# The relative-position bias tile of a hybrid decoder step: built through DRAM rows at a skewed pitch, first of all, in place of a matmul flip

## The chip, the cores and the metric

The kernel runs on one core of a Trainium2 chip. The metric is the device time in microseconds of one execution. A core has five engines that work side by side on queues of their own: TensorE (PE, matmuls; its weight loads are a lane of their own, PEld), VectorE (DVE), ScalarE (ACT), GpSimd (POOL) and SyncE (SP), which here only issues DMAs. ACT issues some DMAs as well. Each engine takes its instructions in the order of its queue and waits on semaphores of the others.

## The reference

One inference step of a two-layer decoder trunk, for 1024 prompt tokens and 64 sample tokens. Layer 0 is differential attention with eight heads beside a spatial gating MLP; layer 1 is gated linear attention. All inputs are float32. What the change touches is the bias that is added to the scores of layer 0:

```python
def t5_bucket(dist):
    n = jnp.maximum(dist, 0)
    max_exact = N_BUCKETS // 2          # 32 buckets
    nf = jnp.maximum(n, 1).astype(jnp.float32)
    large = max_exact + (jnp.log(nf / max_exact) / math.log(MAX_DISTANCE / max_exact)
                         * (N_BUCKETS - max_exact)).astype(jnp.int32)
    large = jnp.minimum(large, N_BUCKETS - 1)
    return jnp.where(n < max_exact, n, large)

s = jnp.einsum('bqhcd,bkhcd->bhcqk', q, k).astype(jnp.float32)
bias = rel_bias[t5_bucket(q_pos[:, None] - k_pos[None, :])]
s = s + jnp.transpose(bias, (2, 0, 1)).astype(jnp.float32)[None, :, None]
s = jnp.where(causal, s, -jnp.inf)
p = jax.nn.softmax(s, axis=-1)
a = p[:, :, 0] - lam * p[:, :, 1]
```

The bias depends only on the head and on the distance between query and key, and is the same for all distances of 128 and more. So, less its last value (which a softmax doesn't see), it is zero outside a band, and one tile of 128 query rows by 256 keys for each head holds it for every block of queries, with a large negative number where the key lies after the query.

## The kernel before

The prompt is worked in eight tiles of 128 tokens, and the 64 sample tokens are the ninth (NT = 9). Layer 0 starts with a loop over 72 units, head by head and in each head tile by tile (lines 465 to 507). In step s the loop emits the projection of unit s (`qkv_tile`, 24 matmuls), and for earlier units the transposes (2 steps back), the scores (5 back), the softmax times values (6 and 8 back) and the output transposes (12 back). Ahead of the loop stand `xprep` of the first four x tiles (load, normalise, transpose, split in a high and a low part), `load_head(0)` (the weights of head 0, eight DMAs of 192 KB through four buffers) and `small_consts`. `xprep` has two buffers for loaded tiles.

The program's order gives each instruction a priority. A planner with a model of the times (`schedule_with_timeline_sim`) then lays out the queue of each engine: an instruction that is ready in the model may pass one of higher priority that isn't. On the chip the order of a queue is fixed.

The bias tile `tb` (128 partitions x 8 heads x 256) is made by `bias_setup` (lines 208 to 230), called in step s = 1. Three small loads (`rel`, `r31`, `oh`; lines 213 to 215) bring the table, its last row and a one-hot matrix. DVE subtracts (L216), TensorE makes a row of 384 bias values for each head, running from distance 255 down (L218), DVE copies it to SBUF as `bsb`, 8 x 384 (L220), and SP writes it to DRAM as `bias_d` (L221). Two DMAs read it back into `rev` with a step of one element from partition to partition (L226), so partition p holds the row shifted by p. This is `tb` with its partitions in reverse, and a matmul with a reversed identity (`flip`, loaded at L223) turns it round, four times 512 columns (L229), each followed by a DVE copy into `tb` (L230).

`scores` adds `tb` to the scores on DVE (L405). `bias_sample` (L235) copies rows of `tb` into `biasS` for the sample tokens, 16 small DMAs on SP, in steps 20 to 27 of the program.

Of the kernel before, what the change touches and what calls it, by code (L numbers as in the profile page):

```python
# [10 lines left out]
F32 = mybir.dt.float32  # L11
# [13 lines left out]
P = 128  # L25
KT = D // P
H = 8
# [10 lines left out]
PRM = {'ktc': 'a', 'ev': 'p', 'ekm': 'p', 'qem': 'd', 'gm': 2, 'wp': (3, 6), 'at': 'a', 'LQ': 2, 'LS': 5, 'LA': 6, 'L2': 8, 'LO': 12, 'on': 'a', 'oT': 'a', 'qk4': 'p', 'kh': 'd', 'vt': 'a', 'qkc': 'a', 'sq': 'p', 'kg': 'p', 'at0': 'a', 'at1': 'a', 'qh': 'd', 'onm': 'd', 'TS': True, 'p0': 2, 'p1': 2, 'qkb': 3, 'qhb': 2, 'ksb': 3, 'lpq': 2, 'qd': 'a', 'vb': 16, 'atb': 2, 'onb': 4}  # L38
# [18 lines left out]
VL = 3  # L57
NW = 14
KW = 4
LEVELS = (64, 32, 16, 8, 4, 2, 1)  # L60


# [4 lines left out]
def ap_of(a, off, dims):  # L67
    return bass.AP(a.tensor, a.offset + off, dims)
# [3 lines left out]
def hybrid_step(  # L72
# [1 line left out]
    x_prompt, x_sample, cache_k, cache_v, state_gla, page_table, rel_bias, norm0_g, w_in0,  # L74
    q_norm_g, k_norm_g, lam, subln_g, ln_v_g, ln_v_b, spatial_w, spatial_b, w_out0,
    norm1_g, w_in1, w_gate, b_gate, gla_norm_g, w_out1,
    c_f32, c_onehot, c_lev, c_flip,
    y_prompt, y_sample, k_prompt, v_prompt, k_sample, v_sample, vb_sample, gla_prompt, gla_sample,
):
    nc = tc.nc  # L80
    pe, act, dve, pool = nc.tensor, nc.scalar, nc.vector, nc.gpsimd
# [18 lines left out]

    dram = ctx.enter_context(tc.tile_pool(name="dram", bufs=1, space=DRAM))
    oT_d = dram.tile([2 * KT, P, T], F32, name="oT_d")
    bias_d = dram.tile([H, 384], F32, name="bias_d")
    vb_d = dram.tile([T + NS, D], F32, name="vb_d")
    v_d = dram.tile([T, D], F32, name="v_d")
    g_d = dram.tile([T, D], F32, name="g_d")
# [9 lines left out]
    cf = const([P, 326], "cf")  # L116
# [66 lines left out]
    if True:  # L183
# [24 lines left out]
        def bias_setup(pp, ps, tb):  # L208
            rel = pp.tile([33, H], F32, name="rel", bufs=1)
            r31 = pp.tile([32, H], F32, name="r31", bufs=1)  # L210
            oh = pp.tile([33, 384], F32, tag="on", name="oh", bufs=PRM["onb"])
            dve.memset(rel[32:33, :], BIG)
            nc.sync.dma_start(rel[0:32, :], rel_bias)
            nc.sync.dma_start(r31, rel_bias[31:32, :].broadcast_to([32, H]))
            nc.sync.dma_start(oh, c_onehot)
            dve.tensor_tensor(rel[0:32, :], rel[0:32, :], r31, ALU.subtract)  # L216
            bps = ps.tile([P, 512], F32, tag="t", name="bps", bufs=3)
            pe.matmul(bps[:H, :384], rel, oh, start=True, stop=True)  # L218
            bsb = pp.tile([H, 384], F32, tag="on", name="bsb", bufs=PRM["onb"])
            dve.tensor_copy(bsb, bps[:H, :384])  # L220
            nc.sync.dma_start(bias_d, bsb)  # L221
            flip = pp.tile([P, P], F32, tag="on", name="flip", bufs=PRM["onb"])
            nc.sync.dma_start(flip, c_flip)  # L223
            for q in range(2):
                rev = pp.tile([P, 4, 256], F32, tag="p1", name=f"rev{q}", bufs=PRM["p1"])
                nc.sync.dma_start(rev, ap_of(bias_d, q * 4 * 384, [[1, P], [384, 4], [1, 256]]))  # L226
                for u in range(2):
                    bps = ps.tile([P, 512], F32, tag="t", name=f"bfl{q}_{u}", bufs=3)
                    pe.matmul(bps, flip, rev[:, u * 2:u * 2 + 2, :], start=True, stop=True)  # L229
                    dve.tensor_copy(tb[:, q * 4 + u * 2:q * 4 + u * 2 + 2, :].rearrange("p h k -> p (h k)"), bps)  # L230

        def bias_sample(tb, h):
            for c in range(2):
# [27 lines left out]
        with ExitStack() as p1:  # L261
            pa = p1.enter_context(tc.tile_pool(name="pa", bufs=2))
            ps = p1.enter_context(tc.tile_pool(name="ps1", bufs=2, space=PSUM))
# [27 lines left out]
            def xprep(i):  # L291
                r = rows(i)
                xt = pa.tile([P, D], F32, tag="xt", name=f"xt{i}", bufs=2)
                nc.sync.dma_start(xt[:r], x_rows(i))
                if i == 0:
                    nc.scalar.dma_start(gbc, norm0_g.broadcast_to([P, D]))
                    nc.sync.dma_start(cf, c_f32)
                xn = pa.tile([P, D], F32, tag="at", name=f"xn{i}", bufs=PRM["atb"])
                ss = pa.tile([P, 1], F32, tag="ss0", name=f"ss0_{i}")
                act.activation(xn[:r], xt[:r], AF.Square, accum_out=ss[:r])  # L300
                rs = pa.tile([P, 1], F32, tag="rs0", name=f"rs0_{i}")
                rsqrt(rs[:r], ss[:r], 1, 1.0 / D)
                dve.scalar_tensor_tensor(xn[:r], xt[:r], rs[:r], gbc[:r], ALU.mult, ALU.mult)
                for half in range(2):
                    tp = ps.tile([P, 512], F32, tag="t", name=f"xtp{i}_{half}", bufs=3)
                    tv = tp.rearrange("p (k t) -> p k t", k=4)
                    for k in range(4):
                        kk = half * 4 + k
                        pe.transpose(tv[:, k, :r], xn[:r, kk * P:(kk + 1) * P], ident[:r, :r])
                    o = (i % 3) * P  # L310
                    hs = xh[i // 3][:, half * 4:half * 4 + 4, o:o + r]
                    ls = xl[i // 3][:, half * 4:half * 4 + 4, o:o + r]
                    split(hs, ls, tv[:, :, :r])
                    if i == NT - 1:
                        pool.tensor_copy(xs[:, half * 4:half * 4 + 4, :NS], f32(hs))
                        pool.tensor_copy(xs[:, half * 4:half * 4 + 4, NS:], f32(ls))
# [136 lines left out]
            def load_head(h):  # L453
                Ws[h] = load_w(w_in0, 0, [(s * D + h * P, P) for s in range(3)], f"wq{h}", PRM['lpq'] if h else 4)

            wp = ps.tile([P, 512], F32, tag="t", name="wp", bufs=3)
            for _ in range(NW):
                pe.matmul(wp[:, :P], ones, ones, start=True, stop=True)
            xprep(0)
            load_head(0)  # L460
            xprep(1)
            small_consts()
# [22 lines left out]
            for s in range(len(units) + max(8, PRM['LO'] + 1)):  # L485
                if s == len(units) - 2:
                    load_gate(0)
                stage(s, PRM['LO'], otr)
                stage(s, PRM['L2'], av2)
                stage(s, PRM['LA'], av)  # L490
                stage(s, PRM['LS'], scores)
                stage(s, PRM['LQ'], qk_trans)
                if 0 <= s - 1 < len(units) and units[s - 1][1] == NT - 1:
                    stage(s, 1, qkv_post)
                if 1 <= s <= NT - 4:
                    xprep(s + 3)
                if s == 1:
                    bias_setup(pa, ps, tb)
                if 20 <= s < 20 + H:
                    bias_sample(tb, s - 20)  # L500
                if s < len(units):
                    h, i = units[s]
                    if i == 3 and h + 1 < H:
                        load_head(h + 1)
                    st_[h, i] = qkv_tile(h, i, Ws[h])
                elif s - len(units) < NPRE:
                    gate_a(*du[s - len(units)], gate_tiles)
# [384 lines left out]
    with ExitStack() as p4:  # L892
# [516 lines left out]
        for n in range(NT - 1):  # L1409
            tb = TB[n]  # L1410
# [28 lines left out]
def _constants():  # L1439
    cf = np.zeros((P, 326), np.float32)  # L1440
    cf[:, 0:P] = np.eye(P)
    for h in range(H):
        for c in range(2):
            for q in range(8):
                r = (h % 4) * 32 + (h // 4) * 16 + c * 8 + q
                cf[r, 128 + (h % 4) * 32 + (h // 4) * 8 + q] = 1.0
                cf[r, 320 + c] = 1.0
    b = np.arange(NS) // 8
    cf[:NS, 256:320] = b[:, None] == b[None, :]
    part = np.arange(P) // 8 % 4  # L1450
    cf[:, 322] = np.where(part == 1, -1.0, 1.0)
    cf[:, 323] = part == 1
    cf[:, 324] = np.where(part == 2, -1.0, 1.0)
    cf[:, 325] = part == 2
    n = np.arange(256)
    nf = np.maximum(n, 1).astype(np.float32)
    large = 16 + (np.log(nf / np.float32(16)) / np.float32(math.log(8.0)) * np.float32(16)).astype(np.int32)
    bucket = np.where(n < 16, n, np.minimum(large, 31))
    oh = np.zeros((33, 384), np.float32)
    for e in range(384):  # L1460
        dist = 255 - e
        oh[bucket[dist] if dist >= 0 else 32, e] = 1.0
    lev = np.zeros((P, len(LEVELS), 64), np.int32)
    s = np.arange(P)[:, None]
    for li, hf in enumerate(LEVELS):
        m = np.arange(64)[None, :]
        t = (m // hf) * 2 * hf + hf + m % hf
        lev[:, li, :] = (s // (2 * hf) == t // (2 * hf)) & (s % (2 * hf) < hf)
    return {"c_f32": cf, "c_onehot": oh, "c_lev": lev, "c_flip": np.ascontiguousarray(np.eye(P, dtype=np.float32)[::-1])}


_INS = ["x_prompt", "x_sample", "cache_k", "cache_v", "state_gla", "page_table", "rel_bias", "norm0_g", "w_in0",
# [23 lines left out]
```

## Time and profile before

| what | value |
|---|---|
| median of 3 runs | 1801.37 us (1799.54 to 1802.87) |
| profiled execution, span from first to last instruction | 1806.1 us |
| instructions | 31855 |
| PE busy | 1747.1 us, 97% |
| DVE busy | 1012.4 us, 56% |
| ACT busy | 755.4 us, 42% |
| POOL busy | 609.3 us, 34% |
| mean granted TensorE clock | 0.991 of full |

No time beside its span is given for the profiled execution; the span is 4.7 us above the median. Times below are from the start of the span. [...] In the timeline, a number in brackets is how long the engine was idle before the instruction, with what ended that.

### The profile page before, as it was taken

The numbers are of one execution on the slowest core, as the hardware profiler recorded it, in microseconds if no ns is written. First come the engines' busy times: TensorE is split into PE (matmuls) and PEld (weight loads), VectorE is DVE, ScalarE is ACT, GpSimd is POOL, SyncE is SP. The second block draws the span as 40 slices with busy tenths as digits, with TensorE's granted clock in tenths as the row PEclk, the third lists the DMA queues.
The fourth block names the chain that finished last, engine by engine and source line by source line (L and its number), as shares of the span: only waits on it lengthen the run. The fifth ranks groups of instructions, "written<-read, shape, count | busy, mean of one in ns | idle before, by whom it ended". The sixth has DMA issues, their size and how long they took to land.

```text
span 1806.1 us, 31855 instructions
## 1 busy us (share of the span) xinstructions
PE 1747.1 (97%) x11429; PEld 1629.0 (90%) x11429; DVE 1012.4 (56%) x2223; ACT 755.4 (42%) x1934; POOL 609.3 (34%) x893
## 2 busy tenths in 40 slices
PE   7999999999999899999899999999999999998999
PEld 6798999999999888889899999999999999996777
DVE  5898888988983233223832342444354455667442
ACT  4566656666664222223222232333343334345241
POOL 4555646655653221112721200044111232235230
PEclk8999999999999999999999999999999999999999
DMA  7102202211213766746221262432334244438741
GB/s 211 52 23 73 68 20 67 67 43 43 66 59 104 243 202 232 236 165 213 59 79 54 92 199 74 129 97 82 94 116 152 80 126 123 130 111 260 240 130 71
DMA packets 223302, 211.62 MB, mean 117 GB/s; under 512 B 22286, under 2 KB 201143, under 8 KB 223143
## 3 DMA queue, kind: packets, MB, share of 16 engines
q1 hardware_dynamic: 203510, 194.35, 34.7%
q10 hardware_dynamic: 19632, 15.21, 2.8%
q8 instruction: 91, 1.49, 0.4%
q14 instruction: 69, 0.56, 0.1%
HBM read 151.35 MB, written 56.24 MB: 115 GB/s over the span
## 4 chain that ended last, share of the span: by engine, by line
PE 62%; DVE 16%; DMA 9%; ACT 4%; POOL 4%; issue 4%; SPq 0%; ACTq 0%; POOLq 0%; DVEq 0%
PE o L1373 5%; PE yo L143 3%; PE yo L145 3%; PE yo L144 3%; PE vg L143 3%; PE vg L144 3%; PE vg L145 3%; DMA oT_d<-oTr 2%; DVE p L418 2%; PE zv L143 1%; PE zv L144 1%; PE zv L145 1%; PE o L434 1%; PE s L399 1%; PE qkv L143 1%
## 5 line engine op out<-in xcount | busy, mean ns | idle before, releaser
L412 ACT ACTIVATE p<-s,nm 128x256 f32<-128x256 f32 (+7 forms) x128 | 95.0, 747 | 38.3 <-DVE nm L409 22.3
L399 PE MATMUL s<-ks,qs 128*128 128x512 f32 (+3 forms) x384 | 96.5, 364 | 2.8 <-DVE ks L384 1.4
L87 ACT CAST qs<-qs 64x256 fp32r<-64x256 f32 x128 | 51.7, 404 | 76.8 <-DVE qs L381 74.2
L1120 POOL TENSOR_TENSOR e<-e,k 128x256 f32<-128x256 f32 (+1 forms) x50 | 42.4, 853 | 117.1 <-ACT e L1117 100.8
L338 POOL TENSOR_TENSOR sq<-qk 128x256 f32<-128x256 f32 (+1 forms) x72 | 46.9, 652 | 95.0 <-ACT qk L87 94.2
L434 PE MATMUL o<-v,at 128*128 128x128 f32 x576 | 76.8, 279 | 1.6 <-ACT at L87 1.6
L399 PEld LDWEIGHTS s<-ks,qs 128*128 128x128 f32 x384 | 64.9, 190 | 12.6 <-ACT p L412 2.8
L434 PEld LDWEIGHTS o<-v,at 128*128 128x128 f32 x576 | 71.4, 193 | 4.2 <-ACT at L87 2.6
L131 POOL TENSOR_TENSOR s<-s,mhalf 128x4 f32<-128x4 f32 (+1 forms) x72 | 73.3, 1018 | 5.3
L837 DVE TENSOR_TENSOR yp<-yp,yo 128x384 f32<-128x384 f32 (+1 forms) x48 | 25.3, 530 | 74.5 <-ACT yp L836 41.7
L407 DVE TENSOR_REDUCE nm<-s 128x1 f32<-128x640 f32 (+3 forms) x64 | 65.2, 1019 | 1.2
L747 POOL TENSOR_TENSOR u<-u,th 128x384 f32<-128x384 f32 (+1 forms) x24 | 28.7, 1194 | 99.9 <-DVE th L746 99.4
L405 DVE TENSOR_TENSOR s<-s,tb 128x256 f32<-128x256 f32 (+1 forms) x128 | 52.8, 412 | 8.9 <-PE s L399 5.6
L418 DVE SCALAR_TENSOR_TENSOR p<-p,fac,p 128x128 f32<-128x128 f32 (+3 forms) x64 | 55.1, 861 | 1.7
L1373 PE MATMUL o<-w1h,oh 128*128 128x512 f32 x128 | 53.0, 414 | 2.5 <-ACT oh L1350 2.5
L87 ACT COPY at<-atp 128x512 f32<-128x512 f32 (+2 forms) x96 | 44.5, 481 | 20.0 <-PE atp L427 19.8
L746 DVE SCALAR_TENSOR_TENSOR th<-th,gb 128x384 f32<-128x384 f32 (+1 forms) x24 | 12.6, 524 | 69.0 <-ACT th L745 69.0
L1373 PE MATMUL o<-w1l,oh 128*128 128x512 f32 x128 | 50.8, 397 | 0.0
L1373 PE MATMUL o<-w1h,ol 128*128 128x512 f32 x128 | 50.3, 407 | 0.0
L427 PE MATMUL atp<-cf,p 128*128 128x128 f32 x288 | 46.8, 275 | 1.9 <-DVE p L418 1.8
L343 POOL TENSOR_TENSOR qk<-qk,s 128x256 f32<-128x256 f32 (+1 forms) x72 | 46.6, 647 | 4.7
L381 DVE SCALAR_TENSOR_TENSOR qs<-qkt,qg,qs 64x128 fp32r<-64x128 f32 x128 | 44.5, 348 | 3.6
(825 smaller groups left out, 6340.4 us busy)
## 6 DMA issues: line engine op xcount, KB each, us to landing
kp<-in_cache_k SPq DMA_DIRECT2D x32, 512.0 KB
vp<-in_cache_v SPq DMA_DIRECT2D x32, 512.0 KB
or<-oT_d SPq DMA_DIRECT2D x16, 384.0 KB
vb_d<-zs SPq DMA_DIRECT2D x36, 128.0 KB
oT_d<-ob SPq DMA_DIRECT2D x8, 544.0 KB
gt<-g_d SPq DMA_DIRECT2D x34, 128.0 KB
xt<-in_x_prompt SPq DMA_DIRECT2D x8, 512.0 KB
out<-v ACTq DMA_DIRECT2D x64, 64.0 KB
```

Source lines behind the costliest of these rows:

```text
L87: act.activation(o, i_, AF.Copy, scale=scale) if scale is not None else act.copy(o, i_)
L131: pool.tensor_tensor(dst, dst, mhalf[:dst.shape[0], :n], ALU.pow)
L143: pe.matmul(out, lh, rh, start=(s == 0), stop=False)
L144: pe.matmul(out, lh, rl, start=False, stop=False)
L145: pe.matmul(out, ll, rh, start=False, stop=(s == n - 1))
L399: pe.matmul(sc[c][:, k0:k0 + w], qs[:, c, l], kts[h, j][:, c, :w], start=(l == 0), stop=(l == 1))
L405: dve.tensor_tensor(sc[c][:, lo:n], sc[c][:, lo:n], tb[:, h, 256 - (n - lo):], ALU.add)
L407: dve.tensor_reduce(nm[:, c:c + 1], sc[c][:, :n], axis=AX.X, op=ALU.max, negate=True)
L412: act.activation(pc[:, :n], sc[c][:, :n], AF.Exp, bias=nm[:, c:c + 1], accum_out=ss[:, c:c + 1])
L418: dve.scalar_tensor_tensor(pt[0][:, :n], pt[1][:, :n], fac, pt[0][:, :n], ALU.mult, ALU.add)
L434: pe.matmul(op[:, :P], at[:, j * P:(j + 1) * P], vts[h, j], start=(j == 0), stop=(j == i))
L1373: pe.matmul(it.mp[:r], lh[:, k, :r], rh[k][:, cs], start=(k == 0 and a == 0), stop=(k == KT - 1 and a == 2))
```

## The change

The row `bsb` is written to DRAM 128 times for each head, one copy behind the other at a pitch of 385 elements (SH), in one DMA from ACT's queue whose source repeats. One DMA on SP's queue then reads `tb` at a pitch of 384, beginning at element 127: partition p begins at 127 + 384 p, which is element 127 - p of copy p. So the tile arrives the right way round, and the flip, its constant, its four pairs of matmuls and the four copies are gone. `bias_setup` is called right after `xprep(0)`, ahead of `load_head(0)`, in place of step s = 1.

```diff
+SH = 385
-    bias_d = dram.tile([H, 384], F32, name="bias_d")
+    bias_d = dram.tile([H, P * SH], F32, name="bias_d")
             bsb = pp.tile([H, 384], F32, tag="on", name="bsb", bufs=PRM["onb"])
             dve.tensor_copy(bsb, bps[:H, :384])
-            nc.sync.dma_start(bias_d, bsb)
-            flip = pp.tile([P, P], F32, tag="on", name="flip", bufs=PRM["onb"])
-            nc.sync.dma_start(flip, c_flip)
-            for q in range(2):
-                rev = pp.tile([P, 4, 256], F32, tag="p1", name=f"rev{q}", bufs=PRM["p1"])
-                nc.sync.dma_start(rev, ap_of(bias_d, q * 4 * 384, [[1, P], [384, 4], [1, 256]]))
-                for u in range(2):
-                    bps = ps.tile([P, 512], F32, tag="t", name=f"bfl{q}_{u}", bufs=3)
-                    pe.matmul(bps, flip, rev[:, u * 2:u * 2 + 2, :], start=True, stop=True)
-                    dve.tensor_copy(tb[:, q * 4 + u * 2:q * 4 + u * 2 + 2, :].rearrange("p h k -> p (h k)"), bps)
+            nc.scalar.dma_start(ap_of(bias_d, 0, [[P * SH, H], [SH, P], [1, 384]]), bsb[:, None, :].broadcast_to([H, P, 384]))
+            nc.sync.dma_start(tb, ap_of(bias_d, 127, [[SH - 1, P], [P * SH, H], [1, 256]]))
@@
             xprep(0)
+            bias_setup(pa, ps, tb)
             load_head(0)
@@
-                if s == 1:
-                    bias_setup(pa, ps, tb)
```

## Rows read from the trace of the kernel before

**Rows 1.** The page: busy us, share of the span and instructions of each engine.
```profile
PE 1747.1 (97%) x11429; PEld 1629.0 (90%) x11429; DVE 1012.4 (56%) x2223; ACT 755.4 (42%) x1934; POOL 609.3 (34%) x893
```

**Rows 2.** Windows of 10 us: length, busy PE, PEld, DVE, ACT, POOL; clock, DMA share, GB/s.
```profile
10.00:20.00 10.00, 8.61 (x44) 7.16 (x43) 9.23 (x20) 7.80 (x17) 3.75 (x6) 0.83 0.91 254
20.00:30.00 10.00, 9.24 (x59) 8.97 (x58) 7.36 (x11) 6.00 (x14) 7.99 (x12) 1.00 0.76 227
30.00:40.00 10.00, 8.45 (x38) 7.20 (x36) 4.40 (x6) 2.06 (x5) 5.64 (x12) 0.83 0.28 83
40.00:50.00 10.00, 7.28 (x14) 3.21 (x14) 2.79 (x5) 0.49 (x3) 0.04 (x1) 0.66 0.47 131
50.00:60.00 10.00, 9.96 (x64) 9.93 (x65) 9.07 (x23) 6.16 (x14) 6.82 (x13) 1.00 0.10 28
```

**Rows 3.** The chain that ended last, around the bias tile: start, us, what.
```profile
34.35 4.11 DMA bias_d<-bsb
38.48 4.01 DMA rev<-bias_d
```

**Rows 4.** Timeline of the engines, 6 to 58 us: start, us, engine, line, operation.
```profile
6.13 1.06 ACT L300 ACTIVATE xn<-xt 128x1024 f32<-128x1024 f32 x1 [3.38 <-DMA xt<-in_x_prompt]
10.93 0.62 PE L143 MATMUL qkv<-wq0h,xh 128*128 128x384 f32 x1 [0.24 <-ACT xh L135]
19.01 0.44 PE L144 MATMUL qkv<-wq0l,xh 128*128 128x384 f32 x1 [0.59 <-DVE wq0l L175]
33.68 0.45 PE L143 MATMUL qkv<-wq0h,xh 128*128 128x384 f32 x1 [1.24 <-ACT v L87]
34.25 1.53 DVE L303 SCALAR_TENSOR_TENSOR xn<-xt,rs,gbc 128x1024 f32<-128x1024 f32 x1
42.62 6.62 PE L229 MATMUL bfl<-rev,flip 128*128 128x512 f32 x8 [2.94 <-DMA rev<-bias_d]
49.09 0.27 PE L364 MATMUL qkt<-cf,qk 128*128 128x128 f32 x1
57.30 0.28 DVE L405 TENSOR_TENSOR s<-s,tb 128x128 f32<-128x128 f32 x1
```

**Rows 5.** SP's queue in order of time, DMA issues: start, us, line, transfer, count.
```profile
1.72 2.62 SPq L172 DMA_DIRECT2D wq0r<-in_w_in  x4
10.04 1.81 SPq L172 DMA_DIRECT2D wq0r<-in_w_in  x3
11.89 0.47 SPq L213 DMA_DIRECT2D rel<-in_rel_bias  x1
15.14 0.36 SPq L294 DMA_DIRECT2D xt<-in_x_prompt  x1
39.51 0.58 SPq L294 DMA_DIRECT2D xt<-in_x_sample  x1
45.42 7.62 SPq L235 DMA_DIRECT2D biasS<-tb  x11
```

**Rows 6.** Groups by line, first 60 us: count, busy us, mean ns of one.
```profile
L216 DVE TENSOR_TENSOR rel<-rel,r 32x8 f32<-32x8 f32 x1 | 1.0, 997 | 0.0
L218 PE MATMUL bps<-oh,rel 33*8 33x384 f32 x2 | 0.8, 484 | 0.0
L220 DVE COPY bsb<-bps 8x384 f32<-8x384 f32 x1 | 0.5, 536 | 0.0
```

**Rows 7.** DMA view: ACT's queue (q10) in 730.4:731 and 703.65:704.5; the copy's size.
```profile
q10 hardware_dynamic: 13, 0.03, 13.7%
...
q10 hardware_dynamic: 9, 0.03, 14.0%
...
vn<-vsm ACTq DMA_DIRECT2D x8, 32.0 KB
```

**Rows 8.** DMA view of 2 to 6 us: queue, packets, MB, share of 16 engines.
```profile
q1 hardware_dynamic: 288, 0.63, 45.8%
q10 hardware_dynamic: 144, 0.52, 35.6%
```

More of the change, by code (lines that the diff above doesn't have):

```diff
@@ L76, in hybrid_step @@
     norm1_g, w_in1, w_gate, b_gate, gla_norm_g, w_out1,
-    c_f32, c_onehot, c_lev, c_flip,
+    c_f32, c_onehot, c_lev,
     y_prompt, y_sample, k_prompt, v_prompt, k_sample, v_sample, vb_sample, gla_prompt, gla_sample,
@@ L1468, in _constants @@
         lev[:, li, :] = (s // (2 * hf) == t // (2 * hf)) & (s % (2 * hf) < hf)
-    return {"c_f32": cf, "c_onehot": oh, "c_lev": lev, "c_flip": np.ascontiguousarray(np.eye(P, dtype=np.float32)[::-1])}
+    return {"c_f32": cf, "c_onehot": oh, "c_lev": lev}
 _INS = ["x_prompt", "x_sample", "cache_k", "cache_v", "state_gla", "page_table", "rel_bias", "norm0_g", "w_in0",
```

## The prediction

> **What bounds the kernel now.** I read the page first, then the windows of the first 60 us, the SP queue in order of time, the chain of waits and the DMA view of short stretches. TensorE is busy for 97% of the span [rows 1], so a change outside it counts only where it stops or starts that engine. The windows show where it is not full: 8.61, 9.24, 8.45 and 7.28 us of each ten between 10 and 50 us, and 9.96 from 50 on [rows 2]. The bias tile sits in the worst of these. After the matmul, the 8x384 row goes to DRAM (4.11 us from issue to the next step), comes back as 128 shifted rows (4.01 us), and only then the flip matmuls start [rows 3]. [...] From 39.68 (42.62 less 2.94) to 49.09 it does nothing but this: 9.4 us. DVE, ACT and POOL are busy for 2.79, 0.49 and 0.04 us of that window [rows 2]: they wait for TensorE and have nothing that would step into its place.
>
> **What is removed.** The 9.4 us as a whole. Its successors were ready: the transposes of the first tile need a POOL result of long before, and the projection of tile 4 follows 1.4 us behind them in either kernel. DVE's four copies lay in its own idle time and are no gain of their own. The flip's 64 KB load goes too; I cost it at nothing, as SP waits for the written row right after it. In 30 to 40 us the clock is 0.83 [rows 2]; whether that slow piece stays is open, between 0 and 1.5 us of gain (0.17 of 10 us). I take 0.
>
> **What is moved.** The three small loads now go out before the head's weights: 0.47 us of SP time for one [rows 5], some 1.4 for the weights and the second x tile. The first weight load was issued at 1.72 [rows 5] and ACT's first work on anything loaded is at 6.13 [rows 4], so DMA, not SP, sets this start; cost 0, or 1.4 without that cover. The subtraction (1.0 us on DVE), the two matmuls (0.97) and the copy (0.54) [rows 6] fall before 10 us, where DVE is ahead of its first x tile and TensorE has only warm-up: cost 0, or 0.5 if the copy comes just ahead of the x normalisation. The row is then in SBUF near 9.5 us (loads landed with the first x tile near 6.5, plus 2.5).
>
> **What is added, first the write.** ACT's queue writes 8 x 128 x 384 floats, 1.57 MB, where SP wrote 12 KB. Nothing in the trace has this shape, so I bound it. From below: the rate of a full stretch, 254 GB/s in 10 to 20 us [rows 2], makes 6.2 us. The nearest row is the sample values' copy, 32 KB out of eight partitions on the same queue. In one quiet stretch of 0.6 us its packets took 13.7% of 16 engines, 1.3 us of engine time for 32.8 KB, or 25 GB/s for one engine [rows 7]; eight rows going side by side at that rate would make 200 GB/s and 7.9 us. In another it was 14.0% of 0.85 us, 17 GB/s, or 11.4 us. From above: that whole 32.8 KB needed about these 0.6 us, 55 GB/s, and 1.57 MB at that pace needs 28.8 us. I take 8 to 11, because the packets themselves ran at full engine speed in the quiet stretch; the long end stays for the range. With the 4.11 us that even the 12 KB write needed [rows 3], it lands at 22 to 25 us, or 42 at the long end.
>
> [...]
>
> **Then the read and SP's wait.** The tile is read as 1 MB in one DMA. Its halves were read in before too, the first in 4.01 us; 5.5 us for both is my estimate. It lands at 28 to 31 us. Its first reader, DVE's addition to the scores, runs at 57.30 [rows 4], so 47.9 without the 9.4 us: 17 us of room, and none at the long end (48). The new wait is SP's: its read waits for the write, and everything behind it on that queue waits along, x tiles, the last weights of head 0, key stores and the next head's weights. Where it stands in SP's order, the trace tells only indirectly. In before the x load of the sample tile went out at 39.51 [rows 5], though the slot it needed was free when DVE ended its normalisation at 35.78 (34.25 + 1.53) [rows 4]; the read of the bias row stood ahead of it and waited. So the order is made with shorter DMA times than the chip has, and I expect the new read early, among the loads of 10 to 20 us. I take the fourth x tile (issued at 15.14 [rows 5]) as the first one behind it, with the weights of 10.04 to 11.85 as the bad and a later x tile as the good side. Held to 24, it goes out at 25, has the 1 MB ahead of it and lands near 31; from landing to its first projection matmul a tile needs 4.8 us (6.13 to 10.93 [rows 4]), so 36 against 33.68 before [rows 4]: 2.3 us late.
>
> **Sharing of the DMA engines.** Between 2 and 6 us the two queues run side by side (45.8% and 35.6% of the engines [rows 8]). So loads of 12 to 22 us share with the write; 1.57 MB at 254 GB/s is at most 6.2 us for what lies behind all of it, about half of that for head 0's last weights. TensorE has some 2 us of idle between 20 and 34 us to absorb it (0.76 in one window and 1.24 ahead of tile 3 [rows 2, 4]). Left: about 1. This and SP's wait delay the same tiles, so they don't add in full: 3 us for both, from 0 to 6. The 16 small copies into the sample bias (7.62 us of SP time for the first 11 [rows 5]) come earlier; they fall where x tiles have ten and more us of room, cost 0.
>
> **Sum.** 1806.1 - 9.4 + 3.0 = 1799.7 for the span, that is 6.4 less. The median of the runs shown is 4.7 us below the profiled span; I carry the difference over: 1801.4 - 6.4 = **1795.0**. What is late next is the x tiles, then TensorE itself. Beyond 50 us it is full again, so the shift should reach the end; instructions that land in another order later can add or take 3.
>
> **Rivals.**
> Rival 1, slower: the narrow source is slow for all of the write (55 GB/s) and SP stands behind it. The write lands at 42.4. With the fourth x tile behind the read, it goes out at 43.3, lands behind the 1 MB near 49, its projection starts at 53.7 against 33.68, 20 us late; 9.4 come back with the flip and 1.7 from the slow clock of 30 to 40 us (0.83 [rows 2]): 9 us slower, 1810. With the last weights behind it, some 17 slower; with only the fifth x tile, 3. It decides from where the write lands after 33 us (20 us of data, 79 GB/s). [...] Against: single packets at full engine speed.
> Rival 2, no change: the write takes 15 to 20 us, or a short one holds the weights of head 0. A short write that ends at 23 gives the last weights near 31 in place of 19 (where TensorE used them [rows 4]), 12 late, of which 9.4 and some 4 return (0.76 and 1.55 us of idle and 1.7 of slow clock in 20 to 40 us [rows 2]): -1; with 18 us and the fourth x tile it is -1 to -2. Together -3 to +2: 1801.
> Rival 3, faster still: the write is slow, but the read stands so far back that only late x tiles wait. The tile lands at 48, just when wanted; 9.4 less 1.4: 1793.
> A tile that isn't made without TensorE can't be: the flip's matmuls are deleted.
>
> **How the numbers follow.** Forecast 0.42, rival 1 0.30, rival 2 0.20, rival 3 0.08. A difference below 0.2% (3.6 us) can't be told from no change. Faster by more: 0.37 of the forecast (0.05 of it ends within), 0.02 of rival 2, 0.07 of rival 3: 0.46. Slower: 0.27 of rival 1 and 0.03 of rival 2: 0.30. Within: 0.24. The range runs from all 9.4 and 1 of clock gained (1791) to rival 1 a little past its middle (1811); beyond lie its weights case and little else. The forecast's own range is 1791 to 1799.
>
> **What would show it.** Right: no matmuls on the flip; TensorE full from 35 us on; the bias write from ACT over in 8 to 11 us of data; the first addition of the tile near 50 without a wait. Rival 1 shows as SP standing 20 us at the tile's read, x loads issued after 40, and ACT waiting for an x tile. Wrong would be a write that keeps half of the engines from the weights for longer than it lasts itself, or a tile that DVE waits for at its first addition.

## The result and the profile after

| | median (us) | runs | ratio to before |
|---|---|---|---|
| before | 1800.53 | 1799.54 to 1802.87 | |
| after | 1821.96 | 1820.88 to 1823.45 | 1.0111, 95% interval 1.0096 to 1.0127 |

The change makes the kernel 21.4 us slower. The profiled execution of the changed kernel has a span of 1819.2 us and a time of 1820.88. To see how much of the loss is in the first 60 us, I take one mark in both traces: the first matmul of the gate, with which the loop over heads ends. The timeline of the gate's tile `ga` has it (min, median and max ns, first and last start in us); first before, then after:

```profile
L143 PE MATMUL ga<-xh,wg0h x24: 306/334/442, 527.3 to 550.2; 128*128 128x384 f32 x16, 128*128 128x320 f32 x8
```

```profile
L144 PE MATMUL ga<-xh,wg0h x24: 306/334/446, 547.5 to 570.6; 128*128 128x384 f32 x16, 128*128 128x320 f32 x8
```

It is 20.2 us late. From there to the end of the span the changed kernel needs 1271.7 us, the profiled execution of before 1278.8, and the experiments below between 1268.7 and 1278.2, in an order that I can't explain by what was edited. So the medians are the measure of the time and the mark is the measure of the place; 20.2 of the 21.4 us stand at the mark, so the loss lies ahead of it. Each mark comes from one profiled execution, so how far it scatters from one execution to the next isn't known. Most of the loss is there by 70 us: the projection of x tile 4 (tiles are counted from 0) starts 19.6 us late. Before:

```profile
50.45 0.42 PE L143 MATMUL qkv<-wq0h,xh 128*128 128x384 f32 x1
```

After:

```profile
70.03 0.39 PE L144 MATMUL qkv<-wq0h,xh 128*128 128x384 f32 x1
```

The busy line and the windows of the changed kernel answer [rows 1, 2]:

```profile
PE 1742.4 (96%) x11421; PEld 1629.3 (90%) x11421; DVE 1011.5 (56%) x2219; ACT 753.9 (41%) x1934; POOL 615.7 (34%) x893
```

```profile
10.00:20.00 10.00, 9.49 (x38) 7.28 (x36) 7.41 (x16) 5.45 (x12) 2.32 (x4) 0.68 0.82 194
20.00:30.00 10.00, 0.62 (x2) 0.30 (x2) 0.87 (x3) 1.15 (x2) 1.11 (x3) 0.66 0.61 117
30.00:40.00 10.00, 4.99 (x16) 4.99 (x17) 2.44 (x3) 2.10 (x5) 1.48 (x4) 0.50 0.55 101
40.00:50.00 10.00, 3.80 (x26) 3.20 (x24) 2.57 (x3) 1.07 (x2) 3.40 (x5) 0.84 0.49 89
50.00:60.00 10.00, 2.46 (x8) 2.46 (x9) 2.92 (x5) 3.60 (x8) 2.05 (x5) 0.50 0.67 224
60.00:70.00 10.00, 10.00 (x66) 9.93 (x65) 6.38 (x14) 4.64 (x12) 7.59 (x12) 0.96 0.42 124
```

TensorE is full again from 60 us on, not from 50, and nearly empty between 20 and 30, where it was busy for 9.24 us before. The DMA columns point at the cause: 117 GB/s between 20 and 30 us, and 89 to 101 up to 50, write and loads together, where the loads of before moved at 227 in 20 to 30 us. The chain that ended last, the queue of SP, the timeline and the DMA view answer [rows 3, 5, 4, 7] in turn:

```profile
13.18 33.72 DMA bias_d<-bsb
46.96 5.79 DMA tb<-bias_d
```

```profile
13.82 0.56 SPq L287 DMA_DIRECT2D xt<-in_x_prompt  x1
...
16.87 3.72 SPq L287 DMA_DIRECT2D xt<-in_x_prompt  x1
20.68 9.58 SPq L173 DMA_DIRECT2D wq1r<-in_w_in  x2
46.96 0.37 SPq L223 DMA_DIRECT2D tb<-bias_d  x1
47.42 1.06 SPq L173 DMA_DIRECT2D wq1r<-in_w_in  x2
48.53 1.34 SPq L287 DMA_DIRECT2D xt<-in_x_prompt  x2
```

```profile
27.99 1.06 ACT L293 ACTIVATE xn<-xt 128x1024 f32<-128x1024 f32 x1 [8.64 <-DMA xt<-in_x_prompt]
...
34.01 0.51 ACT L175 CAST wq1h<-wq1r 128x384 fp32r<-128x384 f32 x1 [4.87 <-DMA wq1r<-in_w_in]
34.43 0.36 ACT L88 COPY qk<-qkv 128x256 f32<-128x256 f32 x1
...
35.02 0.69 PE L144 MATMUL qkv<-wq0h,xh 128*128 128x384 f32 x1 [13.92 <-ACT v L88]
...
55.43 1.06 ACT L293 ACTIVATE xn<-xt 128x1024 f32<-128x1024 f32 x1 [12.40 <-DMA xt<-in_x_prompt]
...
56.95 0.37 ACT L88 COPY qk<-qkv 128x256 f32<-128x256 f32 x1
...
57.54 0.69 PE L144 MATMUL qkv<-wq0h,xh 128*128 128x384 f32 x1 [13.56 <-ACT v L88]
...
71.40 0.28 DVE L398 TENSOR_TENSOR s<-s,tb 128x128 f32<-128x128 f32 x1
```

```profile
q10 hardware_dynamic: 64, 0.10, 43.4%
q1 hardware_dynamic: 69, 0.04, 5.8%
```

The write takes 33.7 us from issue to the next step. Its packets run from 15 to 46 us at 0.10 MB in 2 us, as in the last fence (44 to 46 us; q10 is ACT's queue, q1 SP's). SP's read goes out at 46.96; SP's stand in front of it is called the hold below. The first addition of the tile waits for nothing (71.40): no compute engine stood for the bias tile, they stood for x tiles and weights.

TensorE lost its time in two waits, 13.92 and 13.56 us, both for ACT's copy out of the projection's one PSUM buffer. The timeline shows what stood ahead of that copy in ACT's order. First it is the square of x tile 2, issued at 13.82 and not there until 27.99, and then the cast of a weight of head 1. Second it is the square of x tile 4, behind SP's hold. Behind each wait the granted clock is 0.50, in a window with 4.99 and 2.46 us of matmul. At this clock the projection's matmuls begin 0.32 us apart (35.50 to 39.98 us), at a clock of 1.00 they begin 0.17 us apart (40.28 to 41.14 us); by these two numbers the 7.45 us would be about 3.5 us shorter at 1.00, an estimate. What the waits cost is seen from start to start. Before, the projections of x tiles 1 and 2 began so:

```profile
21.35 0.45 PE L143 MATMUL qkv<-wq0h,xh 128*128 128x384 f32 x1 [0.76 <-ACT v L87]
...
26.85 0.42 PE L143 MATMUL qkv<-wq0h,xh 128*128 128x384 f32 x1
```

So tile 1 is 13.7 us late (35.02) and tile 2 is 30.7 us late (57.54). By tile 4 the difference is down to 19.6 us: 11.1 us came back, 9.4 of them the stall at the flip, which the changed kernel doesn't have; the rest, 1.7 us, fits the slow clock of the kernel before at 30 to 40 us (0.83 [rows 2]).

### The profile page after: what moved, and what is told of

It is laid out like the page before. It is cut to its first block, busy times and chain, and to the rows that moved or that the text cites. A ratio compares the mean times of both kernels' runs of the same rounds, so it can differ in the third digit from the quotient of the medians.

```text
span 1819.2 us, 31824 instructions
## 1 busy us (share of the span) xinstructions
PE 1742.4 (96%) x11421; PEld 1629.3 (90%) x11421; DVE 1011.5 (56%) x2219; ACT 753.9 (41%) x1934; POOL 615.7 (34%) x893
## 4 chain that ended last, share of the span: by engine, by line
PE 63%; DVE 16%; DMA 9%; ACT 4%; issue 3%; POOL 3%; SPq 0%; ACTq 0%; POOLq 0%; DVEq 0%
PE o L1365 5%; PE yo L144 3%; PE yo L146 3%; PE yo L145 3%; PE vg L144 3%; PE vg L145 3%; PE vg L146 3%; DMA bias_d<-bsb 2%; PE qkv L144 2%; PE qkv L145 2%; PE qkv L146 2%; PE o L427 2%; DVE p L411 2%; PE zv L144 2%; PE s L392 1%
## 5 line engine op out<-in xcount | busy, mean ns | idle before, releaser
L144 PE MATMUL qkv<-wq0h,xh 128*128 128x384 f32 x64 | 24.7, 387 | 27.8 <-ACT v L88 27.5
```

The source lines that it names most:

```text
L144: pe.matmul(out, lh, rh, start=(s == 0), stop=False)
```

## The experiments

Three explanations stood against each other. The write is slow because its source lies on eight adjacent partitions, and while it lasts the loads crawl beside it; or SP's stand at the read is the loss; or the odd pitch of 1540 bytes makes the write slow. The place in TensorE's order is given for each as the start of the gate (before 527.3, after 547.5). Each ratio is to runs of the kernel before taken beside the experiment (medians 1801.35 for 1 to 4, 1800.89 for 5 to 8, 1799.12 for 9 to 11). The code fences are shortened.

**1. The source on 128 partitions.**

```diff
-pe.matmul(bps[:H, :384], rel, oh, ...)
-bsb = [H, 384]
-dma(bias_d [[P * SH, H], [SH, P], [1, 384]], bsb[:, None, :].broadcast_to([H, P, 384]))
+relw = [33, H, 16]; dve.tensor_copy(relw, rel[:, :, None].broadcast_to([33, H, 16]))
+pe.matmul(bps[:, :384], relw, oh, ...)
+bsb = [P, 384]
+dma(bias_d [[8 * SH, P], [SH, 8], [1, 384]], bsb[:, None, :].broadcast_to([P, 8, 384]))
```

> The changed kernel with one thing altered: the 1.57 MB written are the same rows to the same places, but the source lies on 128 partitions (each head's row on 16 of them, made by the same one matmul with a table of 128 columns; each partition is the source of 8 copies) in place of 8 partitions with 128 copies. The order of SP's queue is the same. Theory (narrow source: the write is slow because its source lies on eight partitions, and it slows the loads that share engines with it): the write's data pass in 5 to 9 us in place of 31, x tiles land on time, no TensorE gap over 3 us after 20 us, about 1794 us (1789 to 1800). Rival 1 (the unaligned rows in DRAM, pitch 1540 bytes, make the write slow): still about 30 us of write and 1822 us. Rival 2 (moving the work ahead of the weights is what costs, whatever the write takes): over 1812 us although the write is short.

Measured: 1801.46 us, ratio 1.0005 (0.9992 to 1.0018), gate at 530.0. The same bytes now pass between 16 and 28 us, longer than the 5 to 9 that I expected, and SP reads the tile at 27.49. The slow source is worth 17.5 us of the 20.2 at the mark. But the time is that of the kernel before, not the 1789 to 1800 of the expectation.

**2. Eight source partitions again, four apart (0, 4, ..., 28).**

```diff
+relw = [33, H, 4], matmul to bps[:32], bsb = [32, 384]
-bsb[:, None, :].broadcast_to([H, P, 384])
+bsb[0:32:4, None, :].broadcast_to([H, P, 384])
```

> As the changed kernel, but the eight source rows lie on partitions 0, 4, 8 to 28 in place of 0 to 7 (the matmul makes each row four times, DVE copies 32 rows). Same bytes, still eight source partitions and an outermost dimension of eight. Narrow source as a matter of where the partitions lie (several share one way out of SBUF): the write's data pass in 8 to 12 us, 1793 to 1803 us. Narrow source as a matter of how many partitions or engines take part: still about 30 us, 1822 us. Rival 1 (unaligned rows in DRAM): still about 30 us, 1822 us.

Measured: 1802.58 us, ratio 1.0011 (0.9990 to 1.0033), gate at 530.1; packets between 16.5 and 29.3 us. The DMA view of 24 to 26 us, to be held against the fence of the changed kernel above:

```profile
q10 hardware_dynamic: 190, 0.29, 38.6%
q1 hardware_dynamic: 190, 0.09, 15.6%
```

The count of rows and the size of the packets are those of the changed kernel, and both queues together fill about half of the sixteen engines in both (49.2% and 54.2%). But a packet of the write needs 38.6% of 32 us (16 engines, 2 us) over 190, 65 ns, where it needed 43.4% of 32 over 64, 217 ns. So the number of engines isn't the cause of the slow write; which partitions it reads is. (The planner also laid out SP's queue a little differently here and in 9: x tile 3 goes out ahead of the first weight of head 1. That bears on the mark, not on the time of a packet.)

**3. A pitch of 512 elements.** `SH = 512`: the rows of 1536 bytes begin every 2048 bytes, and the read steps by 511 elements.

> The changed kernel with SH = 512 in place of 385: rows are written at a pitch of 2048 bytes, so that each begins aligned, and read at a pitch of 511 elements. Bytes, descriptors, source and queue order unchanged. Narrow source: the write takes 31 us as before, 1822 us within 4. Rival 1 (unaligned rows in DRAM): the write drops under 15 us and the time under 1803 us.

Measured: 1819.49 us, ratio 1.0111 (1.0088 to 1.0134), gate at 548.5; the write goes from 15 to 46 us as before the edit. So the pitch isn't what makes the write slow.

**4. The kernel before, with the write alone put in early.** Its result is used by nobody; the flip stays.

```diff
             xprep(0)
+            bias_write(pa, ps)      # row as in the changed kernel, then ACT's write to an own DRAM tile
             load_head(0)
```

> The kernel before, plus the change's early part up to and with the 1.57 MB write from eight partitions, into a DRAM tile that nobody reads; the bias tile is still made by the flip at its old place. So SP never waits for the write. Theory that loads crawl beside the write (its engines serve the two queues in turn): the third and fourth x tile land 10 us and more late although they were issued in time, 1811 to 1824 us. Rival 3 (the loss is SP's wait at the read of the tile, with loads not yet issued behind it): x tiles land on time, 1800 to 1804 us.

Measured: 1828.35 us, ratio 1.0167 (1.0141 to 1.0193), gate at 552.1, 24.8 late, and beyond the 1811 to 1824 that I expected. SP waits for nothing of the write here. Its queue in order of time, TensorE's wait, and the DMA view of 36 to 38 us:

```profile
14.26 4.90 SPq L215 DMA_DIRECT2D rel<-in_rel_bias  x1
19.20 4.57 SPq L216 DMA_DIRECT2D r<-in_rel_bias  x1
23.81 4.09 SPq L217 DMA_DIRECT2D oh<-in_c_onehot  x1
28.01 4.98 SPq L174 DMA_DIRECT2D wq1r<-in_w_in  x1
33.08 4.95 SPq L311 DMA_DIRECT2D xt<-in_x_prompt  x1
45.79 2.05 SPq L174 DMA_DIRECT2D wq1r<-in_w_in  x4
```

```profile
47.34 0.69 PE L145 MATMUL qkv<-wq0h,xh 128*128 128x384 f32 x1 [17.47 <-ACT v L88]
```

```profile
q10 hardware_dynamic: 67, 0.10, 44.6%
```

The write beside the loads is enough for a loss of this size here: SP's queue moves 0.01 to 0.03 MB in 2 us between 18 and 28 us, and its issue instructions themselves take 4.09 to 4.98 us, where those of 0.80 to 2.79 us in the same run take 0.40 to 0.56. The hold isn't needed for it. Part of the 24.8 us may belong to this kernel alone, though: the three small loads of the old set-up stand in SP's queue from 14.26 to 27.90, ahead of x tile 3 and the first weight of head 1, whose cast at 46.34 is what ACT's copy stood behind. In the changed kernel no such loads stand there.

The last fence is a stretch in which SP moved nothing: the write still takes 213 ns for a packet. It isn't slowed by the loads; they are slowed by it. In the slowest stretches of the changed kernel (28 to 30 and 40 to 46 us) SP's queue passes about one packet for each of the write's (69 to 64 in the fence further up), and its packets are smaller: 0.04 MB in 2 us beside 0.10. In others it passes more; from 26 to 28 us:

```profile
q10 hardware_dynamic: 66, 0.10, 41.9%
q1 hardware_dynamic: 250, 0.14, 25.1%
```

Why it is about one for one in some stretches and not in others isn't shown: no view here tells the engine of a packet.

**5. The wide source, and no hold for x tiles.** As 1, but the read may go out only when x tile 4 was squared.

```diff
+                if i == 4:
+                    pool.tensor_copy(tb[0:1, 0, 0:1], ss[0:1])   # and only then the read of tb
```

> The wide source of the first experiment, and the read of the table is made to wait for x tile 4 as well (a one-element copy from its sum of squares into the table's corner), so that SP has issued x tiles 4 and 5 and the last weights before it stands. Nothing is left out. Theory (the 9.4 us of the flip's stall were given back at SP's hold, 17.5 to 27.5 us in the wide run): x tile 4 is issued by about 26 us as before, the third qkv tile starts by 34 us, and 4 to 9 us come off: 1792 to 1797. Rival (the 1.5 MB more in the first 40 us hold up the weights and x tiles themselves, whatever SP's order): 1800 to 1803.

Measured: 1800.95 us, ratio 0.9996 (0.9985 to 1.0007), gate at 526.8. The read goes out at 37.16, behind the loads of x tiles 4 and 5, and yet they are issued only at 29.19:

```profile
17.80 10.21 SPq L173 DMA_DIRECT2D wq1r<-in_w_in  x4
29.19 2.58 SPq L292 DMA_DIRECT2D xt<-in_x_prompt  x2
```

Four issues of weights took 10.2 us, where before four took 2.62 [rows 5]; in 20 to 30 us the DMA share is 1.00 at 243 GB/s. The time is the rival's (1800 to 1803), not the 1792 to 1797 expected without the hold. At the mark the hold was worth 3.2 us (530.0 to 526.8); in time, the intervals of 1 and 5 overlap. That the rest of what the wide kernel gives back is the 1.57 MB beside the loads is argued from that share of 1.00 and not shown by a run.

**6 and 7. The whole set-up in the old place (step s = 1),** 6 with the wide source, 7 as in the changed kernel:

```diff
-            xprep(0)
-            bias_setup(pa, ps, tb)
+            xprep(0)
@@
+                if s == 1:
+                    bias_setup(pa, ps, tb)
```

> The wide source in the old place (at the second qkv tile), read behind it; nothing is left out. The row set in SBUF at about 40 us as before, write 11 us, read 5.5 us: table at 57 to 59 us, against the first use of the table at 57.3 us before. Theory: no load is behind it except the sample's, PE has no flip in its order, so between nothing and 5 us come off: 1796 to 1802. Rival (a write of 1.5 MB disturbs whatever stands beside it): 1805 or more.

> The changed method unaltered (eight adjacent source partitions) in the old place, at the second qkv tile; nothing is left out. Write of 31 us from about 41 us, read 5.5 us: table at about 78 us, 20 us behind the first use of before. Theory: the price now is the wait for the table, about 20 us less what PE can do meanwhile (5 to 9 us): 1812 to 1821. Rival (the harm is only that the x tiles and weights crawl beside the write, and here few loads are left): 1800 to 1805.

Measured: 6 gives 1796.77 us, ratio 0.9981 (0.9967 to 0.9995), gate at 520.3; 7 gives 1821.55, ratio 1.0128 (1.0110 to 1.0146), gate at 544.1. So the method without the flip is worth 7.0 us at the mark, once the write is quick and nearly all x loads and weights are out before it. With the narrow source the loss is about as large as in the early place (1821.55 for 1821.96 us, 16.8 for 20.2 at the mark), but made otherwise. The timeline of 7:

```profile
35.98 11.36 ACTq L351 DMA_DIRECT2D out<-v  x1
47.38 0.40 ACT L88 CAST qs<-qs 64x256 fp32r<-64x256 f32 x1 [10.84 <-issue]
...
75.51 0.30 DVE L398 TENSOR_TENSOR s<-s,tb 128x128 f32<-128x128 f32 x1 [18.74 <-DMA tb<-bias_d]
```

Now the tile itself is late: DVE stands 18.74 us for it. And ACT stood for 10.84 us at the issue of a small store, behind the write on its own queue.

**8. The old method in the early place.** The flip stays; `bias_setup` of the kernel before is called behind `xprep(0)`.

> The old method (flip by matmul) moved to the place of the changed kernel, behind x tile 0; nothing is left out. This is the position alone. 12 KB and twice 512 KB pass instead of 1.5 MB and 1 MB, and SP stands behind a 12 KB write only. Theory: the stall of 9.4 us at 39.7 us goes, SP stands about 4 us in front of x tile 3 and PE 0 to 4 us at the flips: 1792 to 1798. Rival (any work put in the first 30 us delays the loads by as much as it saves): 1800 to 1805.

Measured: 1798.50 us, ratio 0.9994 (0.9981 to 1.0007), gate at 520.6. The early place alone brings 6.7 us at the mark, although the flip costs TensorE 5.37 us there. In the time, the interval takes in no change. Its difference to 5 is 6.2 us at the mark. 1.57 MB at the 254 GB/s of a full stretch [rows 2] would be 6.2 us as well, but that the numbers are equal is luck: 5 has neither the flip nor its copies, and a gate on its read, so the bytes alone aren't priced by this pair.

**9. Eight source partitions, two apart (0, 2, ..., 14),** otherwise as 2.

> The changed kernel with its eight source rows on partitions 0, 2, ..., 14 in place of 0 to 7 (the sums are made for 16 rows, every other one is written from); place, order and bytes are as in the changed kernel, nothing is left out. Theory (the write is as fast as its source partitions have ways out of SBUF, and the loss is as long as the write, since the loads crawl beside it): between the 31 us of step 1 and the 12.8 us of step 4, some 16 to 20 us, and in time a third to a half of the way from step 4 to step 1: 1806 to 1812. Rival (the eight source rows must lie in separate groups of four, or only the number of DMA engines counts): 31 us again and 1820 to 1824, or 12 to 13 us and 1800 to 1804.

Measured: 1805.48 us, ratio 1.0036 (1.0024 to 1.0049), gate at 532.0; packets between 14 and 30 us. The DMA view of 20 to 22 us:

```profile
q10 hardware_dynamic: 132, 0.20, 45.7%
q1 hardware_dynamic: 274, 0.21, 32.4%
```

45.7% of 32 us over 132 is 111 ns for a packet, half of the changed kernel's 217. The three DMA views have the write at 0.10, 0.20 and 0.29 MB in 2 us for steps of 1, 2 and 4: twice the spread gave twice the rate here, and the next doubling less than that. Why it gave less isn't shown. In 9 itself, from 24 to 26 and from 26 to 28 us, a packet takes 66 and 65 ns, as at step 4, with 16.2% and 31.1% of the engines filled by the write:

```profile
q10 hardware_dynamic: 79, 0.12, 16.2%
...
q10 hardware_dynamic: 153, 0.24, 31.1%
```

From 22 to 24 us it takes 100 ns, with 30.6% filled, so the share alone doesn't tell the pace. 65 ns, 24 GB/s for one engine, is about the quickest that 1536 bytes went in 2 and 9; the copy in [rows 7] made 25. The expectation for the time was a little too high: the loss doesn't grow in proportion (12.8 us of write cost 2.8 at the mark, 16 us 4.7, 31 us 20.2); the slack of the x tiles may be why.

**10 and 11. The wide source with the set-up behind x tile 2 (10) or x tile 3 (11).** One line moved.

```diff
             xprep(2)
+            bias_setup(pa, ps, tb)      # 10; in 11 behind xprep(3)
             xprep(3)
```

> The wide source (128 partitions) with the whole set-up placed between the two places tried: behind the preparation of x tile 2; SP's read of the table comes behind x tiles 2 to 5 and all first-stage weights. Nothing is left out. Theory (no load behind the hold, and the table is there before the first use at about 49 us): the end of the head loop comes at least as early as with the old place (520 us), 1792 to 1797. Rival (the write of 1.5 MB beside x tiles 3 to 5 holds them up as in the early place): 1799 to 1803.

> As the one before, the set-up placed behind the preparation of x tile 3, one place later. Theory: the write starts some us earlier than in the old place, and the 4.9 us that PE stood at 51 us there for the table goes: 1791 to 1796. Rival (the wait for the table was covered by the later stages anyway): 1796 to 1799, no better than the old place.

Measured: 10 gives 1795.95 us, ratio 0.9981 (0.9967 to 0.9995), gate at 520.6; 11 gives 1795.38, ratio 0.9976 (0.9960 to 0.9992), gate at 518.8. Both beat before and after, if by little, and 11 is 8.5 us ahead of before at the mark, where the flip's stall was 9.4. Its gate, read and first use:

```profile
L144 PE MATMUL ga<-xh,wg0h x24: 306/334/444, 518.8 to 542.0; 128*128 128x384 f32 x16, 128*128 128x320 f32 x8
```

```profile
38.19 0.38 SPq L225 DMA_DIRECT2D tb<-bias_d  x1
...
44.75 0.30 DVE L400 TENSOR_TENSOR s<-s,tb 128x128 f32<-128x128 f32 x1 [1.27 <-DMA tb<-bias_d]
```

The write is issued at 29.09, behind the weights and all but two of the x loads, and DVE waits for the tile for 1.27 us only, against 4.78 in 6. The gain in time (3.4 and 4.3 us by the ratios) is less than at the mark; whether the rest is given back behind 520 us or lies in the scatter of the stretch behind it (1268.7 to 1278.8 us) isn't settled. Nor is it shown that the new method beats the old one moved early: 8 and 10 start the gate at the same time, 520.6, and the interval of 8 overlaps those of 10 and 11.

The loss at the mark in steps, each between two kernels that were run: the old method moved early -6.7 (before to 8), its 12 KB made 1.57 MB from a wide source, the flip taken out and the read set back +6.2 (8 to 5), the read put forward again, with the hold, +3.2 (5 to 1), the narrow source +17.5 (1 to after): 20.2.

## Why the prediction was wrong, point by point

- **What bounds the kernel, and the 9.4 us removed: right.** The 9.4 us are TensorE's wait for the row and the flip behind it, up to the transpose at 49.09 [rows 4]. The stall is gone in every kernel without the flip, and in 11, with a quick write behind the urgent loads, the gate starts 8.5 us earlier than before.
- **What is moved: nearly.** The row was in SBUF at 13.2 us, not 9.5: on TensorE its two matmuls came behind the transposes of x tile 0 (9.34 to 11.2). The copy took 0.55 us as before [rows 6]. The first projection starts at 12.50 against 10.93 [rows 4], 1.6 us late, where I took 0 (and named 1.4 and 0.5 as possible). Beside the rest this is little.
- **The size of the write: the term that failed first.** I had 8 to 11 us and a long end of 28.8, and chose the short one, as single packets of the 32 KB copy looked quick [rows 7]: 25 GB/s for one engine. That this is an engine's full speed, as I put it, no run shows, and a packet of the write made 7 GB/s (1536 bytes in 217 ns). The write took 31 us, 51 GB/s, near the 55 GB/s that I had taken for the pace of that whole copy. That this came so near is in part luck. The copy goes from SBUF to SBUF, its 55 GB/s are 32.8 KB over a window that I chose, and the stretch wasn't quiet, as SP's queue filled nearly all the engines in the same 0.6 us (`q1 hardware_dynamic: 57, 0.20, 97.4%`). So neither the packets nor the whole of that copy priced eight rows side by side for 31 us; experiments 2 and 9 do, with 217, 111 and 65 ns for a packet.
- **Sharing of the DMA engines: the term that failed most.** I took bytes over a total rate, at most 6.2 us and 1 of it left, 3.0 together with SP's wait. In place of these 3.0 tile 2's projection is 30.7 us late. Experiment 4 loses 24.8 us at the mark without any wait of SP for the write, if with three small loads more in its queue. Nor does a quick write save the term: in 1 the data pass in 12 us, close to the 8 to 11 that I took, and the gate is still 2.7 us late where the sum had 6.4 gained. In the slowest stretches SP's queue kept about one packet to each of the write's (69 to 64 in 2 us), with 217 ns for a packet of the write, so its rate there didn't follow from bytes over a total; why the counts come out so isn't shown. I had named such a write as what would make me wrong (a write that keeps half of the engines from the weights), but not as a rival with a price.
- **The read and SP's wait: the place was right, the price was not.** The read took 5.8 us, where I had 5.5. It stood early, and the first x tile behind it was one later than I took (tile 4). Rival 1 gave 3 us for that case, taking it that a late tile delays its own projection alone. It delayed the next one as well: ACT squares x tile 4 ahead of copying the projection of tile 1 out of the one buffer, so TensorE stood 13.56 us with tile 2 ready and tile 3 loaded and transposed. In the wide kernel 1, where the hold ends at 27.5, it is worth 3.2 us at the mark.
- **The rivals.** Rival 1 had the right side and the first half of the mechanism (slow narrow source, SP standing, x loads after 40, ACT waiting for an x tile), with a landing of 42.4 for 46.9 and 1810 for 1822. Its case with the last weights behind (17 slower) came near in size, by another way. Rival 2, a short write that brings nothing, is what 1, 2 and 5 are: 1801.5, 1802.6 and 1801.0. Rival 3, a slow write whose read stands far back, was not run. The forecast's own 1795.0 is met by 10 and 11 (1796.0, 1795.4), which have a quick write behind the urgent loads: another kernel than the one that was forecast.
- **Left open.** How much of the narrow kernel's loss is the slowed loads and how much the hold isn't split: the first of TensorE's two waits (13.92 us) has loads behind it that were issued before the hold, the second (13.56) a load issued after it, but the narrow write with the read set back was not run. Nor was a read with a descending step over partitions, which would need no copies in DRAM.

## What to carry to other kernels

Cost a DMA by the partitions it reads, not by its bytes: here eight adjacent partitions let 1.57 MB out in 31 us (51 GB/s), the same rows two apart in 16 us (98), and spreading the same rows over 128 partitions with a wider matmul cost TensorE 0.2 us (1.64 for 1.44). A slow transfer charged its neighbours here: in the slowest stretches the other queue passed about one packet for each of the write's (69 to 64 in 2 us), and an x tile whose load was issued at 13.82 us was there at 27.99. Put it where no load is urgent. And where an engine works in order, a late tile is late for everything that stands behind it there (ACT's square of x tile 4 cost TensorE 13.56 us at the projection of tile 2), so follow the order of that engine rather than the data alone.

## What the runs showed of the hardware

- From SBUF to DRAM with rows of 1536 bytes from eight partitions, a packet took 217, 111 and 65 ns at partition steps of 1, 2 and 4, in stretches in which the write filled 43.4%, 45.7% and 38.6% of the sixteen engines. At step 2 it was 65 ns in a stretch in which the write filled 31.1%, and 100 in one in which it filled 30.6%. At step 1, a pitch of 1540 or 2048 bytes in DRAM made no difference (31 us of write in both).
- Beside the write at step 1 the other hardware queue passed, in the slowest stretches, about as many packets as the write (69 to 64 in 2 us, 0.04 to 0.10 MB; 250 to 66 in a better one), and the write itself was about as slow when alone (213 ns for a packet, 217 beside SP's).
- An issue took longer beside the write: 4.09 to 4.98 us on SP in 4, and 11.4 us on ACT in 7, for a small store behind the write on the same queue, where ACT had 10.84 us of idle because of it.
